# First FFN projection of two layers by Strassen's seven products for 18 of 22 chunks

## The chip, the cores and the metric

One core of a Trainium2 chip runs one program. TensorE (PE in the profile) multiplies matrices into PSUM; VectorE (DVE) and ScalarE (ACT) do elementwise work and can read PSUM; GpSimd (POOL) does elementwise work on SBUF; SyncE (SP) issues the DMAs. The metric is the device time of one execution in microseconds (us), as the median of several runs.

## The reference

A hybrid block of two layers is followed by a second block of two layers, all on 512 positions of width 1024. Each layer of the second block ends in the part that is changed, a feed-forward network (FFN) with a gated convolution:

```python
def conv_ffn(x, w_up, conv_w, conv_b, w_down):      # x 512x1024, w_up 1024x5632, w_down 2816x1024
    a, g = jnp.split(x @ w_up, 2, axis=-1)           # 2816 value columns, 2816 gate columns
    g = causal_depthwise_conv(g, conv_w) + conv_b    # 3 taps along the positions
    return (jax.nn.gelu(g) * a) @ w_down
```

## The kernel before

Every large product is made of three matmuls, since each operand is kept as a high and a low part: the high part is a copy in a rounded 32-bit format (`SC.copy`, ACT), the low part what is left over (`V.tensor_tensor` subtract, DVE). `split` does that for activations and `load_w` for weights: it loads a 128x512 tile `raw` by a DMA of SP's queue (4 buffers) and splits it into a slot `w`. There are 6 weight slots, and `more_w` adds 7 for the FFN, used in turn.

`ffn(l, ...)` is one layer's FFN. The activations stand transposed in `hT`: 8 tiles of 128 model columns by 512 positions, high and low. The 22 chunks of 128 gate columns and 128 value columns are worked in three parts of 8, 7 and 7 chunks, and inside a part in groups of up to four. For a group the gate's 8 weight tiles are loaded (`load_ws`, `K8`), and `fsteps` runs, for each chunk, 8 x 3 matmuls of 512 columns into one PSUM bank of `ps_mm` (4 buffers); then the same for the values. `ev_g` evacuates a gate chunk: ACT scales and adds the bias, DVE adds the two other taps of the convolution, ACT applies GELU. `ev_a` multiplies by the value chunk (DVE) and splits the result into `act` (ACT, DVE). The very first group of a layer runs its gate in two halves of 256 positions, so that it can begin while the last positions are still being normed; its three matmuls stand in lines 1517 to 1519, those of `fsteps` in lines 1060 to 1062.

After a part's groups comes its second projection: `down_part` multiplies `act` by the tiles of `w_down`, in `dsteps` (lines 231 to 233), for two column halves and four blocks of positions, and DVE adds the result to `z` (line 1532). The third part ends in the layer norm, whose rows `lng` and `lnb` are loaded by `rows`.

The instructions of each engine are put in order when the program is built, by a scheduler that follows the program's order where several could run; on the chip each engine then works through its list in that order. `tick`, `later` and `flush` place small pieces of other work between matmuls.

Of the kernel before, what the change touches and what calls it, by code (L numbers as in the profile page):

```python
# [20 lines left out]
S = 512  # L21
# [100 lines left out]
def _body(ctx, tc, nc, a, out, stop):  # L122
# [36 lines left out]
    def ps_t():  # L159
        return psum("t", [128, 4, 128], 2)  # L160
# [1291 lines left out]

    def open_z(l):
# [6 lines left out]
        def rows(i):  # L1460
            lg = [zp.tile([128, D], F32, name=n, bufs=1) for n in ("lng", "lnb")]
            bcast_row(lg[0], a["ln_g_2"][l, i])
            bcast_row(lg[1], a["ln_b_2"][l, i])
            return lg
        return st, z, rows

    def ffn(l, zst, z, rows, opf, est):
# [5 lines left out]
        more_w(f"wf{l}", 7, fst, "left")  # L1473
        cwr = fp.tile([88, 128], F32, name="cwr")
# [6 lines left out]
        for part, nch in enumerate((8, 7, 7)):  # L1481
            act = [fp.tile([128, 2, S], F32R, name="act", bufs=10) for _ in range(nch)]
            for q0 in range(0, nch, 4):
                nq = min(4, nch - q0)
                ge = {}

                def ev_g(j, ps):
                    c = c0 + q0 + j
                    g0 = fp.tile([128, S], F32, name="g0", bufs=2)
                    SC.activation(g0, ps, AF.Identity, scale=cw[:, 2, c:c + 1], bias=cw[:, 3, c:c + 1])  # L1490
                    V.scalar_tensor_tensor(g0[:, 1:], ps[:, :S - 1], cw[:, 1, c:c + 1], g0[:, 1:], op0=OP.mult, op1=OP.add)  # L1491
                    V.scalar_tensor_tensor(g0[:, 2:], ps[:, :S - 2], cw[:, 0, c:c + 1], g0[:, 2:], op0=OP.mult, op1=OP.add)
                    ge[j] = fp.tile([128, S], F32, name="ge", bufs=6)
                    SC.activation(ge[j], g0, AF.Gelu_apprx_tanh)
# [9 lines left out]
                if part == q0 == 0:  # L1504
                    pt = ps_t()
                    PE.transpose(pt[:, 0, :88], cwr, ident[:88, :88])
                    SC.copy(cw.rearrange("p a b -> p (a b)"), pt[:, 0, :88])
                    pss = [ps_mm() for _ in js]
                    for i, r in enumerate(halves):
                        for j, ps in enumerate(pss):  # L1510
                            for k in K8:
                                if i:
                                    flush()
                                else:
                                    tick()
# [560 lines left out]
```

## Time and profile before

| | |
|---|---|
| median of 3 runs | 1966.53 us (1961.64 to 1968.09) |
| profiled execution | 1962.12 us |
| its span, first to last instruction | 1960.3 us |
| mean granted clock of TensorE | 0.991 |
| matmuls | 10240 |
| busy: PE, DVE, ACT, POOL | 1899.6, 1167.4, 782.5, 203.2 us |
| DMA traffic | 206.18 MB, mean 105 GB/s |

The span is what the trace covers; 1.8 us of the execution's own time lie around it. The clock is a share of the full 2.4 GHz. Matmuls overlap, so the busy time of PE says that one was under way, not that PE ran at its peak.

### The profile page before, as it was taken

How to read it: one execution, taken by the hardware profiler on the slowest of the kernel's cores; microseconds unless marked ns; L12 is line 12 of the kernel's file. 1: busy time of each engine (PE TensorE's matmuls, PEld its weight loads, DVE VectorE, ACT ScalarE, POOL GpSimd, SP SyncE). 2: the span in 40 equal slices, each digit the busy share in tenths (PEclk: the TensorE clock that was granted, in tenths of full speed). 3: DMA queues.
4: the chain of work that ended last, by engine and by line, in shares of the span. 5: the costliest groups of instructions: out<-in, count | busy, mean ns of one | idle time of the engine just before them, and what ended most of it. 6: DMA issues, size and time to landing. Idle time of an engine off the chain costs nothing.

```text
span 1960.3 us, 29102 instructions
## 1 busy us (share of the span) xinstructions
PE 1899.6 (97%) x10240; PEld 1540.1 (79%) x10240; DVE 1167.4 (60%) x2892; ACT 782.5 (40%) x1760; POOL 203.2 (10%) x316
## 2 busy tenths in 40 slices
PE   7999899999999999999999999999999999999998
PEld 4777687877888888768888888888778788888886
DVE  5698887475774235687434444645776774344445
ACT  2432454432553345444323333234665543233330
POOL 3011102012101000110000000101441200000001
PEclk9999999989999999999999999999999999999999
DMA  8535425135234233404322332352113042223321
GB/s 275 170 91 179 130 86 160 58 109 155 65 103 143 65 94 118 162 1 128 94 86 86 108 98 85 112 168 86 42 41 130 24 129 92 86 87 107 99 86 69
DMA packets 132872, 206.18 MB, mean 105 GB/s; under 512 B 20866, under 2 KB 57076, under 8 KB 132725
## 3 DMA queue, kind: packets, MB, share of 16 engines
q1 hardware_dynamic: 132724, 204.31, 33.9%
q8 instruction: 81, 1.33, 0.3%
q14 instruction: 67, 0.54, 0.1%
HBM read 194.62 MB, written 14.09 MB: 106 GB/s over the span
## 4 chain that ended last, share of the span: by engine, by line
PE 72%; DVE 6%; POOL 2%; DMA 1%; issue 1%; ACT 1%; POOLq 0%; DVEq 0%; ACTq 0%
PE mm L1060 11%; PE mm L1062 11%; PE mm L1061 11%; PE mm L231 9%; PE mm L233 9%; PE mm L232 8%; PE t L1095 1%; PE t L274 1%; PE o L1854 1%; PE o L1662 1%; PE mm L1924 1%; DVE w L227 1%; DVE z L1152 1%; DMA raw<-in_ffn_w_up_dram 1%; PE o L939 1%
## 5 line engine op out<-in xcount | busy, mean ns | idle before, releaser
L226 ACT CAST w<-raw 128x512 fp32r<-128x512 f32 (+4 forms) x568 | 321.8, 581 | 401.2 <-PE mm L233 172.1
L227 DVE TENSOR_TENSOR w<-raw,w 128x512 fp32r<-128x512 f32 (+4 forms) x560 | 348.4, 643 | 174.4 <-ACT w L226 171.7
L1060 PE MATMUL mm<-hT,w 128*128 128x512 f32 x920 | 367.0, 399 | 0.0
L1062 PE MATMUL mm<-hT,w 128*128 128x512 f32 x920 | 362.4, 394 | 0.0
L1061 PE MATMUL mm<-hT,w 128*128 128x512 f32 x920 | 361.6, 393 | 0.0
L231 PE MATMUL mm<-w,hT 128*128 128x512 f32 (+3 forms) x704 | 278.2, 396 | 1.2 <-ACT hT L243 1.2
L233 PE MATMUL mm<-w,hT 128*128 128x512 f32 (+3 forms) x704 | 263.2, 374 | 0.0
L232 PE MATMUL mm<-w,hT 128*128 128x512 f32 (+3 forms) x704 | 261.5, 371 | 0.5 <-DVE w L227 0.5
L1062 PEld LDWEIGHTS mm<-hT,w 128*128 128x128 f32 x920 | 172.6, 188 | 40.0 <-DVE w L227 0.8
L1060 PEld LDWEIGHTS mm<-hT,w 128*128 128x128 f32 x920 | 172.9, 188 | 39.7 <-ACT w L226 1.1
L1061 PEld LDWEIGHTS mm<-hT,w 128*128 128x128 f32 x920 | 172.9, 188 | 36.1
L231 PEld LDWEIGHTS mm<-w,hT 128*128 128x128 f32 x704 | 139.8, 199 | 30.4 <-issue 6.9
L233 PEld LDWEIGHTS mm<-w,hT 128*128 128x128 f32 x704 | 139.8, 199 | 20.7 <-issue 1.1
L232 PEld LDWEIGHTS mm<-w,hT 128*128 128x128 f32 x704 | 140.1, 199 | 16.8 <-issue 1.8
L231 PE MATMUL mm<-w,act 128*128 128x512 f32 x352 | 139.0, 395 | 0.0
L232 PE MATMUL mm<-w,act 128*128 128x512 f32 x352 | 138.3, 393 | 0.0
L233 PE MATMUL mm<-w,act 128*128 128x512 f32 x352 | 138.2, 393 | 0.0
L1532 DVE SCALAR_TENSOR_TENSOR z<-z,mm 128x512 f32<-128x512 f32 x48 | 33.0, 687 | 109.8 <-PE mm L233 109.8
L1491 DVE SCALAR_TENSOR_TENSOR g<-mm,cw,g 128x511 f32<-128x511 f32 x44 | 33.0, 749 | 100.2 <-ACT g L1490 100.2
L281 POOL TENSOR_SCALAR rp<-mv 128x1 f32<-128x1 f32 x16 | 9.8, 614 | 775.9 <-DVE mv L1146 774.9
L1090 ACT ACTIVATE E<-E,nm 128x128 f32<-128x128 f32 (+3 forms) x128 | 71.6, 560 | 45.5 <-DVE nm L1089 42.8
L1497 DVE TENSOR_TENSOR ge<-ge,mm 128x512 f32<-128x512 f32 x44 | 30.2, 686 | 83.3 <-PE mm L1062 83.3
(433 smaller groups left out, 3060.0 us busy)
## 6 DMA issues: line engine op xcount, KB each, us to landing
raw<-in_ffn_w_up_dram SPq DMA_DIRECT2D x128, 256.0 KB, 2.9
rawm<-in_w_mod_dram SPq DMA_DIRECT2D x96, 256.0 KB, 3.1
raw<-in_ffn_w_down_dram SPq DMA_DIRECT2D x88, 256.0 KB, 3.0
raw<-in_w_in_dram SPq DMA_DIRECT2D x80, 256.0 KB, 2.8
raw<-in_ev_w_in_dram SPq DMA_DIRECT2D x48, 256.0 KB, 3.1
raw<-in_ffn_w_up_dram SPq DMA_DIRECT2D x64, 192.0 KB, 2.4
raw<-in_w_out_dram SPq DMA_DIRECT2D x32, 256.0 KB, 3.0
raw<-in_w_in_dram SPq DMA_DIRECT2D x32, 128.0 KB, 3.5
```

The costliest lines, as they stand in the source:

```text
L226: SC.copy(hi, r)
L227: (eng or V).tensor_tensor(lo, r, hi.bitcast(F32), op=OP.subtract)
L231: PE.matmul(ps, hi, w[:, 0, w0:w0 + n], start=first, stop=False)
L232: PE.matmul(ps, hi, w[:, 1, w0:w0 + n], start=False, stop=False)
L233: PE.matmul(ps, lo, w[:, 0, w0:w0 + n], start=False, stop=last)
L1060: PE.matmul(ps, wh, hi, start=k == ks[0], stop=False)
L1061: PE.matmul(ps, wh, lo, start=False, stop=False)
L1062: PE.matmul(ps, wl, hi, start=False, stop=k == ks[-1])
L1090: SC.activation(E, E, AF.Exp, scale=scale, bias=nm, accum_out=den)
L1491: V.scalar_tensor_tensor(g0[:, 1:], ps[:, :S - 1], cw[:, 1, c:c + 1], g0[:, 1:], op0=OP.mult, op1=OP.add)
L1497: V.tensor_tensor(ge[j], ge[j], ps, op=OP.mult)
L1532: V.scalar_tensor_tensor(hs, hs, R2 if part == 0 else 1.0, ps, op0=OP.mult, op1=OP.add)
```

## The change

The first projection of 18 of the 22 chunks of each layer is computed by quarters with Strassen's scheme. The model columns are halved (k tiles 0 to 3 and 4 to 7), the positions are halved (`LH`, `RH`), and the two column halves are a group's value columns and gate columns. Instead of eight products of quarters there are seven, each of four k tiles by 256 positions, so each product is 4 x 3 matmuls of 256 columns a chunk. They need sums of quarters on both sides.

On the activations' side `sums` builds three sums on DVE and splits them, once a layer, into the unused tile `yT` and a new tile `hx`; `scr` and `c1s` are views of the norm rows `lng` and `lnb` of the mixer before. On the weights' side, `up_quart` loads three of a group's four weight quarters as f32 (`s` and `x` in the four buffers `v0` to `v3`, `y` in four buffers `bq`), and makes the other operands in place: two sums by DMAs of POOL's queue that add while they write (`plus_dma`, and the one after `o3`), two by POOL (`y` plus `x`, and `plus_raw`, for which the fourth quarter is loaded into `raw`). Each of the seven operands is split into four weight slots.

The results are combined as the products end: the accumulator `X` (two banks of `ps_o`) takes products 0, 5, 6 and 3 in turn and is read in between, `W` and `Y` are two banks each of `ps_mm`. `e1` to `e7` are the evacuations; `e7` includes the gate's convolution and GELU (`gate`), `e4` the last product and the split into `act`. The order of products is 0, 1, 4, 5, 2, 6, 3; the last two run chunk by chunk (`byj`), the others k tile by k tile.

The first group of each layer stays as it was. The parts are 8, 8 and 6 chunks. To make room the FFN adds 3 weight slots for 7 and has 8 buffers of `act` for 10. The calls pass `lgs[0]`, the rows of the last norm.

```diff
-    def ffn(l, zst, z, rows, opf, est):
+    def ffn(l, zst, z, rows, lg0, opf, est):
         halves = (slice(0, 256), slice(256, 512))[::-1 if l else 1]
         fst = ExitStack()
         drain(opf)
         est.close()
         fp = pool(f"ff{l}", stack=fst, side="left")
-        more_w(f"wf{l}", 7, fst, "left")
-        cwr = fp.tile([88, 128], F32, name="cwr")
+        more_w(f"wf{l}", 3, fst, "left")
+        cwr = fp.tile([128, S], F32, name="g0", bufs=2)[:88, :128]
+        hx = fp.tile([128, 2, 4, S], F32R, name="hx")
+        scr = lg0[0].rearrange("p (k s) -> p k s", k=2)
+        c1s = [lg0[1][:, S * i:S * i + S].rearrange("p (j s) -> p j s", j=2) for i in range(2)]
         nc.sync.dma_start(cwr[0:66], a["ffn_conv_w_2"][l].rearrange("i (c p) -> (i c) p", p=128))
         nc.sync.dma_start(cwr[66:88], a["ffn_conv_b_2"][l].rearrange("(c p) -> c p", p=128))
         cw = fp.tile([128, 4, 22], F32, name="cw")
         up, down = a["ffn_w_up_2"][l], a["ffn_w_down_2"][l]
         c0 = 0
         st6 = {}
-        for part, nch in enumerate((8, 7, 7)):
-            act = [fp.tile([128, 2, S], F32R, name="act", bufs=10) for _ in range(nch)]
+        LH, RH = slice(0, 256), slice(256, 512)
+
+        def sums(k):
+            h0, l0, h1, l1 = (hT[:, q, kk:kk + 2] for kk in (k, 4 + k) for q in range(2))
+
+            def tt(o, x, y, op):
+                V.tensor_tensor(o, x, y, op=op)
+            t = scr
+            f = lambda v: v.bitcast(F32)
+            tt(t[:, :, LH], f(h1)[:, :, RH], f(h0)[:, :, RH], OP.subtract)
+            tt(t[:, :, RH], f(h0)[:, :, LH], f(h0)[:, :, RH], OP.subtract)
+            tt(t[:, :, LH], t[:, :, LH], f(l1)[:, :, RH], OP.add)
+            tt(t[:, :, RH], t[:, :, RH], f(l0)[:, :, LH], OP.add)
+            for c in (LH, RH):
+                tt(t[:, :, c], t[:, :, c], f(l0)[:, :, RH], OP.subtract)
+            split(yT[:, 0, k:k + 2], yT[:, 1, k:k + 2], t)
+            V.scalar_tensor_tensor(t[:, :, LH], t[:, :, LH], -1.0, f(h0)[:, :, LH], op0=OP.mult, op1=OP.subtract)
+            tt(t[:, :, LH], t[:, :, LH], f(l0)[:, :, LH], OP.subtract)
+            V.scalar_tensor_tensor(t[:, :, RH], t[:, :, LH], -1.0, f(h1)[:, :, LH], op0=OP.mult, op1=OP.subtract)
+            tt(t[:, :, RH], t[:, :, RH], f(l1)[:, :, LH], OP.subtract)
+            split(hx[:, 0, k:k + 2], hx[:, 1, k:k + 2], t)
+
+        SRC = ((hT, 0, LH), (hT, 4, LH), (hx, 0, RH), (hT, 4, RH), (yT, 0, LH), (hx, 0, LH), (yT, 0, RH))
...
+        def up_quart(q0, nq, act):
+            n, np2 = 128 * nq, nq // 2
+            cg = c0 + q0
+            col = (128 * cg, FF + 128 * cg)
+            src = {(i, m): (lambda k, i=i, m=m: up[128 * (4 * i + k):128 * (4 * i + k) + 128, col[m]:col[m] + n])
+                   for i in range(2) for m in range(2)}
+            buf = {}
+
+            def fresh(name, b):
+                for k in range(4):
+                    if name == "y":
+                        buf[name, k] = fp.tile([128, 512], F32, name="bq", bufs=4)[:, :n]
+                    else:
+                        buf[name, k] = vp.tile([128, 512], F32, name=f"v{k}", bufs=1)[:, :n]
+                    nc.sync.dma_start(buf[name, k], src[b](k))
+
+            def operand(name, then=None):
+                ws = []
+                for k in range(4):
+                    wturn[0] = (wturn[0] + 1) % len(wslots)
+                    px, nx = wslots[wturn[0]]
+                    w = px.tile([128, 2, 512], F32R, tag="w", name="w", bufs=nx)
+                    split(w[:, 0, :n], w[:, 1, :n], buf[name, k])
+                    ws.append(w)
+                    if then:
+                        then(k)
+                return ws
+
+            def plus_raw(k):
+                rw = wp.tile([128, 512], F32, tag="raw", name="raw", bufs=4)[:, :n]
+                nc.sync.dma_start(rw, src[1, 0](k))
+                GP.tensor_tensor(buf["y", k], buf["y", k], rw, op=OP.add)
+
+            X = [ps_o() for _ in range(np2)]
+            W, Y = [None] * np2, [None] * np2
+            g2 = [fp.tile([128, 2, S], F32, name="ge", bufs=3) for _ in range(np2)]
+            v3 = lambda ps: ps.rearrange("p (j s) -> p j s", j=2)
+
+            def product(i, ws, bank, start, byj, evac):
+                tile_, k0, cols = SRC[i]
+                order = [(k, j) for k in range(4) for j in range(nq)]
+                if byj:
+                    order = [(k, j) for jj in range(np2) for j in (2 * jj, 2 * jj + 1) for k in range(4)]
+                for k, j in order:
+                    jj = j // 2
+                    if start and k == 0 and j % 2 == 0 and bank[jj] is None:
+                        bank[jj] = ps_mm()
+                    tick()
+                    ps = bank[jj][:, 256 * (j % 2):256 * (j % 2) + 256]
+                    wh, wl = (ws[k][:, q, 128 * j:128 * j + 128] for q in range(2))
+                    hi, lo = (tile_[:, q, k0 + k, cols] for q in range(2))
+                    s0 = start and k == 0 and j % 2 == 0
+                    PE.matmul(ps, wh, hi, start=s0, stop=False, skip_group_check=True)
+                    PE.matmul(ps, wh, lo, start=False, stop=False, skip_group_check=True)
+                    PE.matmul(ps, wl, hi, start=False, stop=False, skip_group_check=True)
+                    if k == 3 and j % 2:
+                        evac(jj, v3(bank[jj]))
+
+            def e1(jj, ps):
+                SC.copy(c1s[jj], ps)
+
+            def e2(jj, ps):
+                V.tensor_tensor(c1s[jj], c1s[jj], ps, op=OP.add)
+
+            def e5(jj, ps):
+                SC.mul(g2[jj][:, :, RH], ps, -1.0)
+
+            def e6(jj, ps):
+                SC.mul(g2[jj][:, :, LH], ps, -1.0)
+
+            def e3(jj, ps):
+                V.tensor_tensor(g2[jj][:, :, LH], g2[jj][:, :, LH], ps, op=OP.subtract)
+
+            def e7(jj, ps):
+                V.tensor_tensor(g2[jj][:, :, RH], g2[jj][:, :, RH], ps, op=OP.subtract)
+                for j in range(2):
+                    gate(cg + 2 * jj + j, g2[jj][:, j], g2[jj][:, j])
+                V.tensor_tensor(g2[jj][:, :, LH], g2[jj][:, :, LH], c1s[jj], op=OP.mult)
+
+            def e4(jj, ps):
+                V.tensor_tensor(g2[jj][:, :, RH], g2[jj][:, :, RH], ps, op=OP.mult)
+                for j in range(2):
+                    d = act[q0 + 2 * jj + j]
+                    SC.copy(d[:, 0], g2[jj][:, j])
+                    V.tensor_tensor(d[:, 1], g2[jj][:, j], d[:, 0].bitcast(F32), op=OP.subtract)
+
+            fresh("s", (1, 0))
+            fresh("y", (0, 0))
+
+            def plus_dma(k):
+                GP.dma_start(buf["y", k], src[0, 1](k), accum_op=OP.add)
+            o1 = operand("y", plus_dma)
+            o2 = operand("s")
+            product(0, o1, X, True, False, e1)
+            fresh("x", (1, 1))
+            o5 = operand("y")
+            product(1, o2, W, True, False, e2)
+            for k in range(4):
+                GP.tensor_tensor(buf["y", k], buf["y", k], buf["x", k], op=OP.add)
+            o6 = operand("y", plus_raw)
+            product(4, o5, Y, True, False, e5)
+            o3 = operand("x", lambda k: GP.dma_start(buf["x", k], src[0, 1](k), accum_op=OP.add))
+            product(5, o6, X, False, False, e6)
+            o7 = operand("x")
+            product(2, o3, Y, False, False, e3)
+            o4 = operand("y")
+            product(6, o7, X, False, True, e7)
+            product(3, o4, X, False, True, e4)
+
+        def gate(c, ps, dst):
+            g0 = fp.tile([128, S], F32, name="g0", bufs=2)
+            SC.activation(g0, ps, AF.Identity, scale=cw[:, 2, c:c + 1], bias=cw[:, 3, c:c + 1])
+            V.scalar_tensor_tensor(g0[:, 1:], ps[:, :S - 1], cw[:, 1, c:c + 1], g0[:, 1:], op0=OP.mult, op1=OP.add)
+            V.scalar_tensor_tensor(g0[:, 2:], ps[:, :S - 2], cw[:, 0, c:c + 1], g0[:, 2:], op0=OP.mult, op1=OP.add)
+            SC.activation(dst, g0, AF.Gelu_apprx_tanh)
+
+        for part, nch in enumerate((8, 8, 6)):
+            act = [fp.tile([128, 2, S], F32R, name="act", bufs=8) for _ in range(nch)]
             for q0 in range(0, nch, 4):
                 nq = min(4, nch - q0)
-                ge = {}
+                if part or q0:
+                    up_quart(q0, nq, act)
+                    continue
+                g2 = [fp.tile([128, 2, S], F32, name="ge", bufs=3) for _ in range(2)]
+                ge = {j: g2[j // 2][:, j % 2] for j in range(4)}
 
...
                 drain(fsteps(load_ws(up, 128 * (c0 + q0), 128 * nq, K8), range(nq), h_rhs, ev_a))
+                for k in (0, 2):
+                    sums(k)
```

## Rows read from the trace of the kernel before

**Rows 1.** The page: span, and busy time of each engine

```profile
span 1960.3 us, 29102 instructions
...
PE 1899.6 (97%) x10240; PEld 1540.1 (79%) x10240; DVE 1167.4 (60%) x2892; ACT 782.5 (40%) x1760; POOL 203.2 (10%) x316
```

**Rows 2.** Windows: length, busy (count) of PE, PEld, DVE, ACT, POOL, clock, DMA share

```profile
889.00:923.00 34.00, 31.73 (x231) 30.09 (x230) 22.10 (x35) 15.89 (x28) 1.45 (x2) 0.95 0.45 132
...
1034.00:1111.00 77.00, 77.00 (x335) 62.61 (x334) 36.66 (x59) 29.83 (x52) 0.00 (x0) 1.00 0.31 93
1111.00:1150.00 39.00, 39.00 (x170) 31.67 (x169) 16.24 (x24) 9.51 (x16) 0.00 (x0) 1.00 0.32 99
```

**Rows 3.** Windows of TensorE alone, inside stages with one shape

```profile
912.00:920.00 8.00, 8.00 (x71) 1.00 0.41 129
...
946.00:982.00 36.00, 36.00 (x157) 1.00 0.32 95
```

**Rows 4.** TensorE groups by shape: xcount | busy us, mean ns | idle before

```profile
L1060 PE MATMUL mm<-hT,w 128*128 128x512 f32 x920 | 367.0, 399 | 0.0
...
L1517 PE MATMUL mm<-hT,w 128*128 128x256 f32 x128 | 36.5, 290 | 4.7 <-ACT w L226 4.6
```

**Rows 5.** Timeline (start us, duration, engine) at the end of a first projection

```profile
985.61 1.67 ACT L226 CAST w<-raw 128x512 fp32r<-128x512 f32 x3
...
986.43 1.89 DVE L227 TENSOR_TENSOR w<-raw,w 128x512 fp32r<-128x512 f32 x3
```

**Rows 6.** Groups of DVE instructions by shape, 922 to 1268

```profile
L227 DVE TENSOR_TENSOR w<-raw,w 128x512 fp32r<-128x512 f32 x95 | 63.7, 689 | 23.4 <-ACT w L226 22.9
...
L1500 DVE TENSOR_TENSOR act<-ge,act 128x512 fp32r<-128x512 f32 x22 | 15.2, 690 | 6.3 <-ACT act L1499 6.2
```

**Rows 7.** Timeline of one chunk's gate, ACT and DVE

```profile
950.60 0.78 ACT L1490 ACTIVATE g<-mm,cw 128x512 f32<-128x512 f32 x1 [1.25 <-PE mm L1062]
...
951.42 0.75 DVE L1491 SCALAR_TENSOR_TENSOR g<-mm,cw,g 128x511 f32<-128x511 f32 x1 [1.33 <-ACT g L1490]
...
952.20 0.75 DVE L1492 SCALAR_TENSOR_TENSOR g<-mm,cw,g 128x510 f32<-128x510 f32 x1
...
953.05 0.63 ACT L1494 ACTIVATE ge<-g 128x512 f32<-128x512 f32 x1 [1.66 <-DVE g L1492]
```

**Rows 8.** Groups of POOL instructions by shape, whole span

```profile
L704 POOL TENSOR_TENSOR d<-d,kF 128x256 f32<-128x256 f32 x14 | 10.9, 779 | 74.2 <-ACT d L702 60.9 <-DVE acc L390 6.3 <-DVE Sg L725 2.9
L1004 POOL TENSOR_TENSOR xo<-xo,sil_a 128x512 f32<-128x512 f32 x8 | 10.7, 1334 | 9.4 <-DVE sil_a L1003 9.4
L227 POOL TENSOR_TENSOR w<-raw,w 128x512 fp32r<-128x512 f32 x8 | 10.4, 1336 | 1.6 <-ACT w L226 1.6
```

**Rows 9.** Timeline around one POOL add beside DVE's work

```profile
601.65 1.63 POOL L1004 TENSOR_TENSOR xo<-xo,sil_a 128x512 f32<-128x512 f32 x1 [0.92 <-DVE sil_a L1003]
...
602.03 0.75 DVE L1005 SCALAR_TENSOR_TENSOR y<-mm,rstd,mod 128x512 f32<-128x512 f32 x1
...
602.69 1.13 DVE L227 TENSOR_TENSOR w<-raw,w 128x512 fp32r<-128x512 f32 x1
```

**Rows 10.** Groups of DVE instructions by shape, whole span: narrow splits

```profile
L227 DVE TENSOR_TENSOR w<-raw,w 128x256 fp32r<-128x256 f32 x48 | 19.8, 432 | 23.9 <-ACT w L226 23.5
```

**Rows 11.** DMA issues of the whole span, last column us to landing

```profile
raw<-in_ffn_w_up_dram SPq DMA_DIRECT2D x128, 256.0 KB, 2.9
...
skB<-rd SPq DMA_DIRECT2D x4, 192.0 KB, 6.5
```

**Rows 12.** Windows of TensorE around two waits for weights

```profile
1588.00:1596.00 8.00, 5.35 (x45) 1.00 0.65 221
...
908.20:911.70 3.50, 3.50 (x19) 0.51 0.51 133
```

**Rows 13.** Timeline of TensorE at those two waits

```profile
907.66 0.39 PE L1517 MATMUL mm<-hT,w 128*128 128x256 f32 x1 [1.98 <-ACT w L226]
...
1592.70 0.39 PE L1517 MATMUL mm<-hT,w 128*128 128x256 f32 x1 [2.65 <-ACT w L226]
```

More of the change, by code (lines that the diff above doesn't have):

```diff
@@ L1451, in out_evac @@
         return ev
+    lgs = [None]
     def open_z(l):
@@ L1460, in rows @@
         def rows(i):
-            lg = [zp.tile([128, D], F32, name=n, bufs=1) for n in ("lng", "lnb")]
+            lgs[0] = lg = [zp.tile([128, D], F32, name=n, bufs=1) for n in ("lng", "lnb")]
             bcast_row(lg[0], a["ln_g_2"][l, i])
@@ L1503, in ffn @@
                 js = range(nq)
[L1504 to L1515, printed above, removed]
-                                wh, wl = (ws[k][:, q, 128 * j:128 * j + 128] for q in range(2))
-                                PE.matmul(ps[:, r], wh, hT[:, 0, k, r], start=k == 0, stop=False)
-                                PE.matmul(ps[:, r], wh, hT[:, 1, k, r], start=False, stop=False)
-                                PE.matmul(ps[:, r], wl, hT[:, 0, k, r], start=False, stop=k == 7)
-                            if i:
-                                ev_g(j, ps)
-                    js = ()
-                drain(fsteps(ws, js, h_rhs, ev_g))
+                pt = ps_t()
+                PE.transpose(pt[:, 0, :88], cwr, ident[:88, :88])
+                SC.copy(cw.rearrange("p a b -> p (a b)"), pt[:, 0, :88])
+                pss = [ps_mm() for _ in js]
+                for i, r in enumerate(halves):
+                    for j, ps in enumerate(pss):
+                        for k in K8:
+                            if i:
+                                flush()
+                            else:
+                                tick()
+                            wh, wl = (ws[k][:, q, 128 * j:128 * j + 128] for q in range(2))
+                            PE.matmul(ps[:, r], wh, hT[:, 0, k, r], start=k == 0, stop=False)
+                            PE.matmul(ps[:, r], wh, hT[:, 1, k, r], start=False, stop=False)
+                            PE.matmul(ps[:, r], wl, hT[:, 0, k, r], start=False, stop=k == 7)
+                        if i:
+                            ev_g(j, ps)
                 drain(fsteps(load_ws(up, 128 * (c0 + q0), 128 * nq, K8), range(nq), h_rhs, ev_a))
+                for k in (0, 2):
+                    sums(k)
             def a_lhs(t, k):
@@ L2034, in _body @@
         return
-    ffn(0, zst, z, rows, opf, est)
+    ffn(0, zst, z, rows, lgs[0], opf, est)
     if stop == 4:
@@ L2044, in _body @@
         return
-    ffn(1, zst, z, rows, opf, mst)
+    ffn(1, zst, z, rows, lgs[0], opf, mst)
 _INS = ['x', 'c', 'positions', 'w_mod', 'b_mod', 'pre_norm_gain', 'post_norm_gain', 'w_in', 'attn_sinks', 'gla_gate_w',
```

8 lines of the change are left out of this document (1 added, 7 removed).

## Prediction, made before the changed kernel ran

> **What bounds the kernel now.** I read the page's head first: TensorE (PE) is busy 1899.6 of 1960.3 us [rows 1]. A busy PE can still be waiting between overlapping matmuls, so next come the windows of one FFN layer: in the first projection (1034 to 1111) and in the second (1111 to 1150) PE's busy time is the whole window, DVE is at 48% and 42%, ACT at 39% and 24%, POOL does nothing and the DMA engines are a third busy [rows 2]. So in these stages PE alone sets the pace and only fewer PE nanoseconds help, as long as nobody else becomes slower than PE. The reader is to see two paces there: in a stretch that holds only 512-column matmuls 157 of them touch 36.00 us, in one that holds only 256-column matmuls 71 touch 8.00 us [rows 3]. The windows count a matmul that only reaches in, so one duration is added (0.40 and 0.29 us [rows 4]): 36.40 / 157 = 0.232 and 8.29 / 71 = 0.117 us from start to start. The long stretch of rows 2 gives 77.40 / 335 = 0.231. A half-wide matmul costs half, its own weight load included. That matters, since the change makes all its matmuls half-wide.
>
> **PE: removed.** A chunk (128 gate and 128 value columns) is 48 matmuls of 512 columns before, 48 x 0.231 = 11.1 us. With seven products it is 7 x 4 x 3 = 84 of 256 columns, 84 x 0.117 = 9.8 us. A group of four falls from 44.4 to 39.2 us, one of two from 22.2 to 19.6. With 36 chunks in two layers PE's work falls by 36 x 1.28 = 46 us, 2.3%. The parts of 8, 8, 6 chunks for 8, 7, 7 leave the second projection's matmuls the same in number.
>
> **DVE: added.** From rows, back to back: three weight splits end after 1.89 us where one lasts 0.69, so 0.60 each [rows 5]; the other 512-wide tensor_tensor forms have the same mean [rows 6]; the two convolution steps of a chunk take 951.42 to 952.95, 1.53 us [rows 7]. A group of four had 16 splits, 4 products and 4 low parts: 24 x 0.60 + 4 x 1.53 = 20.5 us. Now it has 28 splits (seven operands of four tiles) and 14 others (e2 two, e3 two, e7 four, e4 six): 42 x 0.60 + 4 x 1.53 = 31.3 us, beside PE's 39.2. ACT goes to 28 x 0.53 for high parts [rows 5], 10 further copies or negations at about the same, and 4 x (0.78 + 0.63) for gate and GELU [rows 7]: 25.7 us, no bound.
>
> **POOL: added.** Eight adds of 128x512 a group. The nearest rows are such a two-input add at 1.33 us and POOL's own splits at 1.34 [rows 8], so 10.6 us, alone no bound. But an add and a DVE operation with two SBUF inputs don't run side by side: beside an add at 601.65 that ends at 603.28, the split started at 602.69 takes 1.13 for 0.69 us and ends 0.54 after it, while the DVE operation between them, which reads PSUM, keeps its 0.75 [rows 9]. The add itself takes 1.63 for its usual 1.3. Of DVE's 31.3 us the splits, the low parts, the c1 product and now the convolution too (its input is an SBUF tile where it was PSUM) have two SBUF inputs; only 8 x 0.60 = 4.8 us read PSUM. The split behaves as if it had begun when the add ended. So the price of the adds to DVE lies between 0 (all beside PSUM readers or an idle DVE) and 10.6 us (all in full); with the latter DVE and POOL need 31.3 + 10.6 = 41.9 us together, over PE's 39.2. I take that end less a little, since rows 9 show full exclusion and nothing milder.
>
> The Trainium skill, "SBUF — State Buffer", section "Who interferes with whom", states this as a rule: a Vector instruction with two SBUF inputs and a GpSimd one that reads SBUF exclude each other for a whole instruction. It speaks against giving the weight sums to POOL. By it the adds cost up to their whole 10.6 us; by the delay in rows 9 alone (1.13 for 0.69, 0.44 us a meeting) eight would cost 3.5 us and DVE, at 34.8, would stay under PE.
>
> So a group lasts those 41.9 us, less what overlaps, plus DVE's idle time that neither it nor POOL can use. Overlap I take as 1.9 us, since the adds lie in the middle products and e7 and e4, with half of the PSUM readers, at the end. Idle is sure to come. e7 of the first half can't start before half of product 6 (24 x 0.117 = 2.8 us), and one gate chain runs ACT, DVE, ACT from 950.60 to 953.68, 3.1 us [rows 7]. From mid product 6 to the group's end PE needs 8.4 us. DVE has e7 and e4 of both halves, 2 x (2 x 0.60 + 2 x 1.53) + 6 x 0.60 = 12.1 us, and the next operands: with 9 weight slots the three tiles after the first become free only as product 6 ends. Some 4 us of work are left then. A following group can't start its second bank (X is the accumulator to the last) and a following second projection waits for its last two act tiles. So I take 2.0 us of idle and 42.0 us a group: 2.4 saved of the 5.1. Bounds: 39.2 and 41.9 + 2.8 + 3.1 = 47.8.
>
> **The group of two** has 28 splits 256 wide, about 0.34 back to back (0.43 mean [rows 10] less the 0.09 by which two overlap in rows 5), 7 others at 0.60, two chains of 1.53: 16.8; eight 256-wide adds at 0.78 [rows 8] make 6.2. 23.0 us for 22.2 before: I take 1 us lost.
>
> **DMAs.** 24 transfers of 256 KB a group instead of 16; the engines were a third busy [rows 2]. SP's loads of y wait until the last operand has been split, two products (11 us) ahead, and land in 2.9 us [rows 11]; down loads queued behind them wait as long and have that cover too. The eight adding DMAs go through POOL's queue, each behind a split, with POOL's adds behind them. No such DMA is in the trace: a plain one of the size lands in 2.9, the slowest row in 6.5 us [rows 11]. From the first operand to the third there are two products, 11.2 us; four issues at an add's 1.3 us and 6.5 make 10.4. Nothing, at both ends; uncovered, each microsecond late costs one. The norm row that c1 occupies can be reloaded only after the last e7, in SP's queue ahead of down loads; it is used a whole second projection later, and the loads behind it wait less than the act tiles do: nothing.
>
> **The first group** stays plain, but has 9 slots for 13 and DVE's sums: 20 operations of 0.60 and four 1024-wide low parts of 1.2, 16.8 us a layer. Results are needed in the third product, and DVE is at 22.1 of 34 us in that window [rows 2], so they fit, narrowly: 2 us a layer, between 0 and 16.8.
>
> **The clock.** After an idle of 1.98 us at 905, PE waiting for a weight split, the granted clock was 0.51 from 908.2 to 911.7, that is the lower of its two levels (1.2 GHz), at a loss of 3.5 x 0.49 = 1.7 us; after 2.65 us at 1590 it stayed 1.00 [rows 12, 13]. Of ten ends of groups I let two fall: 3.4 us, between 0 and 17.
>
> **Sum.** 8 groups x -2.4 = -19.2, 2 x +1, 2 x +2, +3.4: -9.8 us. The profiled execution took 1962.1 us (1960.3 and 1.8 around it), so 1952.3; the median of the runs is 4.4 above that execution, so 1957.
>
> **Rivals.** *Cover is better*: adds fall into DVE's waits, groups are PE's 39.2 us and only 1 us is lost at each of ten ends: -46 + 10 + 4 = -32, 1935. For it: DVE's idle time of 8 us in such a group is nearly what the adds need.
> *The shared port decides, slower*: the adds exclude DVE in full and idle reaches 4.5 us, half-way to its bound: 46.4 us a group, 8 x 2.0 + 2 x 3 + 4 + 3.4 = +29, 1996. It turns at 44.4 - 41.9 = 2.5 us of idle without overlap: beyond that a group is slower than the plain one. For it: the end of a group is where DVE has 12 us of work in 8; against: POOL's adds are not due there, with a product or more of slack.
> *Adding DMAs land late*, at 13 us for four instead of 10.4, so each of ten groups waits some 2 us: -9.8 + 20 = +10, 1977. Against: both bounds stay under 11.2.
> *Clock falls at every end*: 17 for 3.4 us, -9.8 + 13.6 = +4, 1970: no change that can be told.
>
> **Chances.** Forecast (1948 to 1965) 0.42, cover better 0.17, port 0.22, late DMAs 0.10, clock 0.09. A measurement here can tell about 0.3%, 5.9 us. Faster: 0.30 of the forecast and the whole second case, 0.47. Same: 0.12 of the forecast, 0.04 of the port, 0.06 of the clock: 0.22. Slower: the rest, 0.31. Range 1932 to 1990: the better cover's centre and nearly the port's.
>
> **What would show it.** Right: 256-column matmuls at 0.117 us in groups; DVE over 75% busy there; splits at 1.1 us beside adds; PE idle at ends of groups, released by DVE's e4 products or by weight splits, some 3 us each, little inside. Wrong: PE waiting inside a group for splits that wait for adding DMAs or adds; sums holding up the first group; a half-clock stretch after each end; weight loads that no longer hide at half width.

## Result: slower by about 1.1%, where a gain of 0.5% was forecast

| | before | after |
|---|---|---|
| median of five runs each | 1965.0 us (1956.7 to 1968.1) | 1983.5 us (1980.1 to 1990.4) |
| ratio, 95% interval | | 1.0109 [1.0075, 1.0143] |
| profiled execution / its span | 1962.1 / 1960.3 us | 1983.5 / 1981.8 us |

The time lies inside the range (1932 to 1990) and on the other side of "before" from the forecast 1957.

**Where it went.** The head of the page after, to be set against [rows 1]:

```profile
span 1981.8 us, 32498 instructions
...
PE 1881.6 (95%) x11536; PEld 1584.9 (80%) x11536; DVE 1354.3 (68%) x3114; ACT 875.9 (44%) x1942; POOL 391.2 (20%) x476
```

PE is busy 18 us less and the span is 21.5 us longer: PE now waits. From the first gate matmul to the last matmul of the second projection the first layer takes 385.7 us (378.9 before) and the second 382.7 (372.7). That is 16.8 of the 21.5; 2.9 more lie after the last matmul (11.3 us, 8.4 before) and the rest ahead of and between the layers. The windows of the changed kernel's groups, columns as in [rows 2]: the lone group and the pair of the first layer, the pair of the second, and then four stretches inside that last pair's second group.

```profile
943.00:986.00 43.00, 40.62 (x337) 39.99 (x336) 32.09 (x40) 23.24 (x41) 16.34 (x12) 1.00 0.59 148
1031.00:1123.00 92.00, 83.78 (x674) 82.64 (x674) 69.54 (x90) 48.93 (x87) 36.63 (x28) 0.96 0.58 139
...
1727.00:1819.00 92.00, 82.91 (x668) 81.81 (x668) 68.89 (x89) 48.22 (x85) 36.62 (x28) 0.96 0.57 139
...
1795.00:1799.00 4.00, 4.00 (x36) 4.00 (x36) 0.00 (x1) 0.00 (x0) 2.37 (x3) 1.00 1.00 176
1799.00:1805.00 6.00, 0.47 (x5) 0.27 (x3) 2.13 (x4) 2.56 (x5) 0.00 (x0) 0.91 0.84 180
1805.00:1809.00 4.00, 3.54 (x16) 3.54 (x17) 3.20 (x6) 3.48 (x7) 0.00 (x0) 0.50 0.64 175
1809.00:1813.00 4.00, 4.00 (x29) 4.00 (x28) 2.87 (x5) 1.30 (x2) 0.00 (x0) 0.78 0.83 272
```

A pair takes 92 us where two plain groups took 88.8, and PE is busy in only 83 to 84 of them. The 36 matmuls in 4.00 us at 1795 are the pace when fed: 0.119 us a matmul with the one-duration correction of [rows 3, 4], 5.7 us a product, 40 us a group. Then PE stands still for 6 us, and for some 6 us more its clock is low: 0.50, the lower of its levels, then 0.78, which costs at most 4 x 0.50 + 4 x 0.22 = 2.9 us.

The waits of TensorE from 890 to 1975 (total us, times, longest) say on whom; L1562 is the first, L1564 the last of the three matmuls that a chunk makes with a weight tile:

```profile
PE o L1562 <- ACT ge L1578: 16.9, 8, 6.0
PE o L1562 <- DVE ge L1584: 7.9, 8, 1.1
PE o L1562 <- ACT w L243: 6.7, 2, 4.1
...
PE o L1564 <- DVE w L244: 2.4, 2, 1.6
PE mm L1562 <- ACT w L243: 2.2, 4, 0.9
PE mm L1564 <- DVE w L244: 1.5, 3, 0.6
```

37.6 us in all, of it 16.9 + 6.7 = 23.6 in front of product 6, which needs the seventh operand o7 and an accumulator that e6 (ACT, L1578) has read. The second group of the second layer's pair shows why it waits, from the timelines of POOL, ACT, DVE and PE:

```profile
1780.55 6.40 POOL L1608 TENSOR_TENSOR bq<-bq,v 128x512 f32<-128x512 f32 x4 [4.48 <-DMA v<-in_ffn_w_up_dram]
1786.91 6.93 POOL L1541 TENSOR_TENSOR bq<-bq,raw 128x512 f32<-128x512 f32 x4
1793.80 3.58 POOL L1611 DMA_DIRECT2D v<-in_ffn_w_up_dram  x4
...
1799.51 0.62 ACT L243 CAST w<-v 128x512 fp32r<-128x512 f32 x1 [8.84 <-DMA v<-in_ffn_w_up_dram]
...
1804.29 0.62 ACT L243 CAST w<-v 128x512 fp32r<-128x512 f32 x1 [0.62 <-DMA v<-in_ffn_w_up_dram]
1804.82 1.08 ACT L1578 ACTIVATE ge<-o 128x512 f32<-128x512 f32 x2
...
1789.22 5.78 DVE L244 TENSOR_TENSOR w<-v,w 128x512 fp32r<-128x512 f32 x4
...
1805.46 0.58 PE L1562 MATMUL o<-yT,w 128*128 128x256 f32 x1 [5.99 <-ACT ge L1578]
```

DVE splits o3 from 1789.22 to 1795.00; as each tile is split, its buffer may take its adding DMA. But POOL works its queue in order, and ahead of these DMAs stand the adds of `plus_raw`, until 1793.8. The four issues take 3.58 us, the landings come up to 1804.3, ACT splits o7 as they land, and e6 waits in ACT's queue behind those splits although its product had ended at 1793.8. The names "ACT" and "e6" in the wait are thus the last link of a chain that runs back to POOL.

Two views of this group alone, of o3's splits (shortest, median and longest in ns) and of x's four adding DMAs, say what the raw adds do to these DMAs:

```profile
L244 DVE TENSOR_TENSOR w<-v,w x4: 680/1776/1780, 1789.2 to 1794.3; 128x512 fp32r<-128x512 f32 x4
...
DMA to landing us min/median/max: 5.6/7.6/8.7
```

The raw adds hold the first DMA in POOL's queue for 2.8 us after its tile has been split, but the last for only 0.5, since o3's last tile is not split before 1795.0. That is late because three of the four splits, beside the raw adds, take 1.78 us and not 0.68. So the raw adds delay the DMAs in two ways, ahead of them in the queue and beside the splits. From the first issue to the last landing the four then take 10.4 us, and product 2 ends 5.7 us after the first issue. The chain does not begin with the raw adds either: POOL stood idle for 4.48 us before its first add, until x's plain load had landed, and SP could issue that only as the second operand, in the same buffers, was split.

The sizes, from the groups by shape (xcount | busy us, mean ns of one) and the DMA issues (xcount, KB, median us to landing) of the whole span:

```profile
L244 DVE TENSOR_TENSOR w<-bq,w 128x512 fp32r<-128x512 f32 x128 | 123.1, 993 | 36.7 <-ACT w L243 35.4 <-PE mm L1564 0.3
L244 DVE TENSOR_TENSOR w<-v,w 128x512 fp32r<-128x512 f32 x96 | 76.7, 824 | 51.1 <-ACT w L243 51.0
L1541 POOL TENSOR_TENSOR bq<-bq,raw 128x512 f32<-128x512 f32 x32 | 55.0, 1750 | 0.0
L1608 POOL TENSOR_TENSOR bq<-bq,v 128x512 f32<-128x512 f32 x32 | 49.2, 1562 | 45.8 <-DMA v<-in_ffn_w_up_dram 40.2 <-DVE w L244 5.6
L1611 POOL DMA_DIRECT2D v<-in_ffn_w_up_dram x40 | 36.0, 1188 | 1.0 <-DVE w L244 0.9
```

```profile
bq<-in_ffn_w_up_dram POOLq DMA_DIRECT2D x32, 256.0 KB, 4.7
v<-in_ffn_w_up_dram POOLq DMA_DIRECT2D x32, 256.0 KB, 6.0
```

Adds take 1.56 and 1.75 us (1.33 in [rows 8]) and splits 0.82 to 0.99 (0.69 in [rows 6]). An adding DMA lands in a median of 4.7 to 6.0 us (2.9 for a plain one in [rows 11]) and costs POOL 36.0 / 40 = 0.90 us to issue.

### The profile page after: what moved, and what is told of

Read it like the earlier page. It is cut to its first block, busy times and chain, and to the rows that moved or that the text cites. A ratio compares the mean times of both kernels' runs of the same rounds, so it can differ in the third digit from the quotient of the medians.

```text
span 1981.8 us, 32498 instructions
## 1 busy us (share of the span) xinstructions
PE 1881.6 (95%) x11536; PEld 1584.9 (80%) x11536; DVE 1354.3 (68%) x3114; ACT 875.9 (44%) x1942; POOL 391.2 (20%) x476
## 4 chain that ended last, share of the span: by engine, by line
PE 51%; DVE 14%; DMA 7%; POOL 5%; issue 4%; ACT 3%; SPq 0%; ACTq 0%; POOLq 0%; DVEq 0%
PE mm L231 7%; PE mm L233 7%; PE mm L232 7%; DMA v<-in_ffn_w_up_dram 5%; PE mm L1060 4%; PE mm L1062 4%; PE mm L1061 4%; DVE w L244 2%; PE t L1095 1%; DVE w L227 1%; POOL bq L1541 1%; DVE g L1622 1%; DMA raw<-in_ffn_w_down_dram 1%; DVE g L1623 1%; PE t L274 1%
## 5 line engine op out<-in xcount | busy, mean ns | idle before, releaser
L227 DVE TENSOR_TENSOR w<-raw,w 128x512 fp32r<-128x512 f32 (+4 forms) x400 | 252.2, 649 | 121.0 <-ACT w L226 119.6
L226 ACT CAST w<-raw 128x512 fp32r<-128x512 f32 (+4 forms) x408 | 231.7, 581 | 214.4 <-PE mm L233 80.4
L244 DVE TENSOR_TENSOR w<-bq,w 128x512 fp32r<-128x512 f32 (+1 forms) x160 | 138.4, 895 | 40.0 <-ACT w L243 38.4
L232 PEld LDWEIGHTS mm<-w,hT 128*128 128x128 f32 x704 | 140.3, 199 | 16.8 <-issue 2.1
L243 ACT CAST w<-bq 128x512 fp32r<-128x512 f32 (+1 forms) x160 | 87.7, 578 | 130.6 <-PE mm L233 57.4
L1060 PE MATMUL mm<-hT,w 128*128 128x512 f32 x344 | 141.1, 411 | 0.0
L1062 PE MATMUL mm<-hT,w 128*128 128x512 f32 x344 | 135.5, 396 | 0.1
L1061 PE MATMUL mm<-hT,w 128*128 128x512 f32 x344 | 135.0, 394 | 0.0
L244 DVE TENSOR_TENSOR w<-v,w 128x512 fp32r<-128x512 f32 (+1 forms) x120 | 89.8, 775 | 61.0 <-ACT w L243 60.7
L1600 POOL DMA_DIRECT2D bq<-in_ffn_w_up_dram x40 | 35.1, 972 | 420.3 <-DVE w L244 324.7
L243 ACT CAST w<-v 128x512 fp32r<-128x512 f32 (+1 forms) x120 | 66.6, 575 | 94.8 <-DMA v<-in_ffn_w_up_dram 79.6
L1562 PE MATMUL o<-hT,w 128*128 128x256 f32 x288 | 82.2, 285 | 8.0 <-DVE ge L1584 7.9
```

Of the source, the lines that this page charges most:

```text
L226: SC.copy(hi, r)
L227: (eng or V).tensor_tensor(lo, r, hi.bitcast(F32), op=OP.subtract)
L232: PE.matmul(ps, hi, w[:, 1, w0:w0 + n], start=False, stop=False)
L243: SC.copy(hi, ps)
L244: V.tensor_tensor(lo, ps, hi.bitcast(F32), op=OP.subtract)
L1060: PE.matmul(ps, wh, hi, start=k == ks[0], stop=False)
```

## Experiments

Twelve kernels. The ratio is that of the runs to the kernel before on the same chip. "Stages" is the sum of both layers' stretches, measured in each trace as above, less the 751.6 us of before: it leaves out what varies elsewhere. It is one execution each; e5's profiled one was 7.4 us under the median of its runs and e1's 2.7 over.

```
kernel                                      median us   ratio [95%]               stages, us
after                                       1983.5      1.0109 [1.0075, 1.0143]    +16.8
e1  x's DMAs ahead of the raw adds          1962.4      1.0002 [0.9981, 1.0023]     -1.8
e2  all sums by adding DMAs                 1972.5      1.0048 [1.0025, 1.0072]     +3.7
e3  POOL's eight adds left out              1941.1      0.9879 [0.9855, 0.9903]    -25.3
e5  e6 ahead of o7's splits                 1974.2      1.0039 [1.0014, 1.0065]     +5.3
f2  e1 and e5                               1958.5      0.9975 [0.9952, 0.9997]     -7.5
f1  e1, e2 and e5                           1982.2      1.0093 [1.0069, 1.0117]    +17.0
f4  f2, groups of two plain                 1946.8      0.9918 [0.9893, 0.9944]    -18.3
e4  x's adding DMAs left out                1938.1      0.9878 [0.9849, 0.9908]    -32.1
g1  x's DMAs plain, same queue              1950.7      0.9951 [0.9932, 0.9970]     -9.5
g2  x's DMAs plain, SP's queue              1955.2      0.9960 [0.9930, 0.9991]    -12.8
g3  the last two sums change places         1944.0      0.9913 [0.9887, 0.9939]    -23.6
g5  g3, e5, plain two, order of 6 and 3     1933.4      0.9866 [0.9842, 0.9891]    -32.8
```

The **queue theory**: x's DMAs are late because of what stands ahead of them in POOL's queue, and everything behind o7 waits. Its rivals as a cause of the loss: the ends of groups, as the forecast had it; the exclusion between POOL's adds and DVE's splits; the landing time of an adding DMA.

### e1, e2, e3, e5: one suspect each

e1 puts the four raw adds behind x's DMAs in POOL's queue:

```diff
-            o6 = operand("y", plus_raw)
+            o6 = operand("y")
             product(4, o5, Y, True, False, e5)
             o3 = operand("x", lambda k: GP.dma_start(buf["x", k], src[0, 1](k), accum_op=OP.add))
+            last = nc.cur_bb.bb.instructions[-1]
+            with tc.issue_after(last):
+                for k in range(4):
+                    plus_raw(k)
```

> Only the order in POOL's queue changes: a group's four adding DMAs into x stand ahead of its four adds of the fourth quarter (plus_raw) instead of behind them. Queue theory (POOL works in order; the DMAs wait there behind adds that DVE's splits stretch to 1.77 us, so o7 is late and product 6 waits): the waits before and inside product 6, some 38 us over the ten groups, mostly go; 1945 to 1960 us. Landing theory (the adding DMA itself, 5.6 us, is too slow wherever it is issued): part of the wait stays, 1965 to 1975. End-of-group theory (DVE's gate and last product set the loss): 1975 to 1985.

e2 makes the other sums by adding DMAs too:

```diff
-                rw = wp.tile([128, 512], F32, tag="raw", name="raw", bufs=4)[:, :n]
-                nc.sync.dma_start(rw, src[1, 0](k))
-                GP.tensor_tensor(buf["y", k], buf["y", k], rw, op=OP.add)
+                GP.dma_start(buf["y", k], src[1, 0](k), accum_op=OP.add)
...
-                GP.tensor_tensor(buf["y", k], buf["y", k], buf["x", k], op=OP.add)
+                GP.dma_start(buf["y", k], src[1, 1](k), accum_op=OP.add)
```

> All four weight sums of a group are made by adding DMAs; POOL adds nothing, so no add shares DVE's SBUF port and nothing but DMA issues stands in POOL's queue. Queue theory: 1940 to 1955 us, splits of DVE back at 0.60 us. Landing theory: y now passes three adding DMAs in series and x one, so it gets worse, 1985 to 2000. End-of-group theory: 1972 to 1983.

e3 leaves out those eight adds and the loads that feed `plus_raw`:

```diff
-                rw = wp.tile([128, 512], F32, tag="raw", name="raw", bufs=4)[:, :n]
-                nc.sync.dma_start(rw, src[1, 0](k))
-                GP.tensor_tensor(buf["y", k], buf["y", k], rw, op=OP.add)
+                pass
...
-            for k in range(4):
-                GP.tensor_tensor(buf["y", k], buf["y", k], buf["x", k], op=OP.add)
```

> POOL's eight adds a group and the load for four of them are left out, so two operands are not the sums that they should be; the adding DMAs stay. Queue theory: the x DMAs go out right behind their splits, 1935 to 1950 us, about as with every sum by DMA. Landing theory: as before, 1975 to 1985. End-of-group theory: 1975 to 1983.

e5 moves e6 ahead of o7's splits in ACT's queue:

```diff
-            o7 = operand("x")
+            neg = [i for i in nc.cur_bb.bb.instructions if i.engine == mybir.EngineType.Activation][-1]
+            with tc.issue_after(neg):
+                o7 = operand("x")
```

> Only ACT's order changes: e6, which product 6 waits for since both use the accumulator X, is put ahead of the splits of o7. Theory of ACT's order (e6 is held up behind splits that wait for DMAs, and that alone makes product 6 late, as the releaser named in the waits says): 1955 to 1965 us. Queue theory: product 6 needs all four tiles of o7 for its first chunk anyway, so no change, 1979 to 1985.

e1 takes back 19 us of stages and e3 42. Only e3's time is inside the queue theory's range. e1 and e5 came out between their cases, and e2 inside the case of the ends of groups, which e3 rules out. In e3 the pair runs at PE's pace, 81 us, with DVE at 69%:

```profile
1618.00:1658.00 40.00, 38.94 (x328) 38.74 (x327) 24.77 (x41) 21.89 (x40) 4.17 (x5) 1.00 0.57 138
1704.00:1785.00 81.00, 80.46 (x674) 79.94 (x673) 56.20 (x89) 48.60 (x86) 10.46 (x12) 1.00 0.56 131
```

The end of a group then costs next to nothing, which takes the forecast's idle off the list. e2 shows that the adds alone are not it: it has none, its splits are back at 0.69 us, and 29 us of e3's gain are missing. Its splits over the whole span, then o3's splits, x's DMAs and their landing in the second group of the second layer's pair:

```profile
L244 DVE TENSOR_TENSOR w<-bq,w 128x512 fp32r<-128x512 f32 x128 | 85.7, 690 | 68.4 <-ACT w L243 68.2
...
1781.50 2.49 DVE L244 TENSOR_TENSOR w<-v,w 128x512 fp32r<-128x512 f32 x4
...
1782.48 3.83 POOL L1609 DMA_DIRECT2D v<-in_ffn_w_up_dram  x4
...
DMA to landing us min/median/max: 5.9/6.9/9.0
```

There o3's splits take 2.49 us, each of x's DMAs goes out 0.3 us behind its split, and PE still waits 3.2 us in front of product 6. What differs from e3 is the landing, 9.0 us for the last (6.9 in e3), and that o3's splits start 1.7 us into product 5 (1.5 us ahead of it in e3). The same views of e1:

```profile
1780.97 2.48 DVE L244 TENSOR_TENSOR w<-v,w 128x512 fp32r<-128x512 f32 x4
...
1782.86 3.58 POOL L1611 DMA_DIRECT2D v<-in_ffn_w_up_dram  x4 [4.17 <-DVE w L244]
...
DMA to landing us min/median/max: 3.9/5.8/8.2
```

With the raw adds behind, o3's splits are back at 2.48 us for four, and POOL stands idle for them. So e1 takes away both ways in which the raw adds delay x's DMAs, as e3 does, and no run here separates the two: that the place in the queue alone was the loss is not shown.

e5 gained 11.5 us of stages (9.3 by the medians), where the queue theory, as first put, had expected nothing. A wait at ACT's splits is then met inside product 6, tile by tile (10.5 us and more for that product in second groups of pairs), and no longer in front of it with e6 behind. The order of ACT's queue was a loss of its own.

### f2, f1, f4: the orders together

f2 is e1 and e5 in one kernel, f1 adds e2's edit. f4 is f2 with the groups of two computed by the plain path:

```diff
-                if part or q0:
+                if (part or q0) and nq == 4:
                     up_quart(q0, nq, act)
                     continue
...
                 js = range(nq)
+                if q0:
+                    drain(fsteps(ws, js, h_rhs, ev_g))
+                    drain(fsteps(load_ws(up, 128 * (c0 + q0), 128 * nq, K8), js, h_rhs, ev_a))
+                    continue
```

> e1 and e5 together: the adding DMAs of x are issued ahead of the raw adds in POOL's queue, and ACT takes e6 ahead of the splits of the seventh operand. POOL's eight adds stay. If the two orders are separate losses (e1 gave 21 us, e5 9 us against the changed kernel), 1983 - 21 - 9 = 1953 us. If ACT's order costs only because the seventh operand is late (queue theory), e1 has taken that already and this stays at e1's 1962. If POOL's adds themselves, stretched by DVE's splits, set the pace (sums of y late, the fourth operand behind them), also 1960 to 1965, with the wait in front of the last product.

> All twelve more sums of a group by adding DMAs, x's ahead of y's last four, and e6 ahead of the seventh operand's splits: no POOL add is left. Queue theory: with the right order nothing is late, groups of four near 40 us as without the adds (e3, 1941), so 1942 to 1950. Landing theory (an adding DMA needs 5.5 us and some 1 us of issue on POOL each, and y's three sums are a chain): the fifth operand of the chain stays late, waits of 2 to 3 us a group remain, 1960 or more.

> f2 with the groups of two (one in each layer) computed plainly, with 512-column matmuls, as in the kernel before. In the changed kernel such a group takes 29 to 30 us against 22.2 plain, so if that loss does not depend on the orders this is 14 us under f2; if the orders have already cured it, up to 5 us over or under f2 (a plain group of two has 2.6 us more of TensorE work).

f2 fell between its two cases: e5's 11.5 us are worth 5.7 on top of e1. f4's plain groups of two are worth 10.8 us of stages, 5.4 each. f1 came out in the range of its second case, slow landing (1960 or more), and undid every gain. Its waits of TensorE (1635 to 1990), and DVE's and PE's timeline at one of them:

```profile
PE o L1560 <- DVE ge L1582: 14.1, 6, 4.5
```

```profile
1807.40 0.69 DVE L244 TENSOR_TENSOR w<-bq,w 128x512 fp32r<-128x512 f32 x1 [0.15 <-ACT w L243]
...
1808.61 0.68 DVE L1582 TENSOR_TENSOR ge<-ge,o 128x512 f32<-128x512 f32 x1
...
1809.43 0.55 PE L1560 MATMUL o<-hT,w 128*128 128x256 f32 x1 [4.46 <-DVE ge L1582]
```

The four DMAs for o4 now go out last and land in 7.0 us (median of all 96 on y), o4's splits wait for them, and e7 (L1582), which product 3 needs, stands behind those splits in DVE's queue. The lateness was handed from one in-order queue to the next.

### e4, g1, g2: x's four transfers

e4 leaves x's adding DMAs out, g1 makes them plain loads at the same place in POOL's queue, g2 plain loads by SP.

```diff
 e4  o3 = operand("x")
 g1  o3 = operand("x", lambda k: GP.dma_start(buf["x", k], src[0, 1](k)))
 g2  o3 = operand("x", lambda k: nc.sync.dma_start(buf["x", k], src[0, 1](k)))
```

> The four adding DMAs on x are left out (the seventh operand is then the third over again, so the output lacks that sum); POOL's adds stay as they are. If the late landing of these DMAs is the loss, all waits in front of product 6 go: 1955 to 1963, as e1 or a little better. If the adds stretch DVE's splits so far that DVE sets the pace, groups stay at 43 us or more: 1973 or more.

> The four adding DMAs on x become plain loads of the same block, at the same place in POOL's queue (the seventh operand lacks the sum). Nothing but the landing changes. If the place in the queue, behind the raw adds, is the loss, some 10 us of the waits in front of product 6 stay when landing is 2.9 us shorter: 1960 to 1970. If the adding itself is slow and the place does not matter: 1938 to 1945, as with these DMAs left out (e4).

> The same four plain loads through SP's queue, not POOL's (the seventh operand lacks the sum). Queue theory: nothing stands ahead of them but the third operand's splits, 1938 to 1945 as e4. If their bytes on the DMA engines, or a wait that holds SP's later loads, were the loss: 1955 or more.

e4, at 1938 us below both of its cases, settles whether the exclusion sets the pace of a group. Its eight adds take 1.55 and 1.77 us, its splits 0.82 and 1.00, as in the changed kernel, DVE is at 86% of a pair, and yet the pair takes 81 us:

```profile
1702.00:1783.00 81.00, 80.49 (x674) 80.09 (x674) 69.41 (x90) 49.50 (x87) 29.78 (x21) 1.00 0.49 133
```

Against e3 the adds cost DVE 69.41 - 56.20 = 13.2 us in a pair, 6.6 a group, and the pair no time. The 48.9 us of stages between e4 and the changed kernel are for the most part found in the latter's 37.6 us of waits (4.5 in the same lines of e4) and at most some 12 us of low clock (1.00 less the granted clock, over the two pairs at 0.96 and the two last parts at 0.98 and 0.95: 3.7 + 3.7 + 1.4 + 3.5; some of it fell while PE stood still and is in the waits already). So x's four adding DMAs, as they are placed, are the loss, and not the adds and the exclusion by themselves, which e4 keeps.

g1 prices the adding: issue falls to 22.2 / 40 = 0.56 us and landing to 4.1.

```profile
L1611 POOL DMA_DIRECT2D v<-in_ffn_w_up_dram x40 | 22.2, 560 | 2.6 <-DVE w L244 1.9
```

```profile
v<-in_ffn_w_up_dram POOLq DMA_DIRECT2D x32, 256.0 KB, 4.1
```

That is 26 us of stages, and 22.6 are left against e4. The time lies between the two cases: neither the late issue nor the adding is the whole; both eat the same slack. The Trainium skill, "DMA: Bandwidth & Descriptors", section "SWDGE vs HWDGE vs iDMA", says that a transfer which accumulates can only be issued from GpSimd; in this kernel all of them are, and no run shows another way.

g2 came out at its upper case. SP's queue is in order too: x's loads stand behind loads of the second projection's weights, and those wait for buffers that the raw adds hold; o3's splits, beside the raw adds, are as late as before. SP's waits from 1755 to 1792:

```profile
SPq L213 <- POOL bq L1541: 14.2, 4, 10.3
```

### g3, g5: the same work, the sums changed about

If slack is the matter, the sum with the tightest due time should have the shortest way. In g3 o4's sum, wanted last, is made by adding DMAs and o7's by POOL adds of a block that SP loads early: the same eight adds, eight adding DMAs and bytes.

```diff
 def plus_raw(k):
-    rw = wp.tile([128, 512], F32, tag="raw", name="raw", bufs=4)[:, :n]
-    nc.sync.dma_start(rw, src[1, 0](k))
-    GP.tensor_tensor(buf["y", k], buf["y", k], rw, op=OP.add)
+    GP.dma_start(buf["y", k], src[1, 0](k), accum_op=OP.add)
+def x_raw(k):
+    rw = wp.tile([128, 512], F32, tag="raw", name="raw", bufs=4)[:, :n]
+    nc.sync.dma_start(rw, src[0, 1](k))
+    GP.tensor_tensor(buf["x", k], buf["x", k], rw, op=OP.add)
...
-o3 = operand("x", lambda k: GP.dma_start(buf["x", k], src[0, 1](k), accum_op=OP.add))
+o3 = operand("x", x_raw)
```

g5 adds e5's order and the plain group of two, and products 6 and 3 take each weight tile for both chunks of a pair before the next:

```diff
-order = [(k, j) for jj in range(np2) for j in (2 * jj, 2 * jj + 1) for k in range(4)]
+order = [(k, j) for jj in range(np2) for k in range(4) for j in (2 * jj, 2 * jj + 1)]
```

> The two sums change places: y's last sum (for the fourth operand, wanted last) is made by adding DMAs, issued as the sixth operand is split, and x's sum (for the seventh operand, wanted two products after the third) by POOL adds of a block loaded early. The same number of adds, adding DMAs and bytes. Queue theory: the tight sum has the short way and the long way has two products of slack, so groups of four near 40 us, the group of two still late: 1945 to 1955. If the amount of POOL work, or the exclusion between its adds and DVE's splits, is the loss: 1975 or more, as nothing of that changes.

> The swap, e6 ahead of the seventh operand's splits in ACT, the two group of two plain, and products 6 and 3 that take the four weight tiles in turn for a pair of chunks. If each of these is a separate loss: groups of four at 40 us or a little under, 8 x 40 + 2 x 22.4 against 2 x 222 before, 1930 to 1940. If the swap has taken all: within 4 us of the swap less the group of two's 7 us a layer.

g3 is 40 us of stages faster than the changed kernel with nothing removed. POOL's timeline in the same group (its adding DMAs are now L1544, its adds for o7 L1541), and the pair's window:

```profile
1754.89 6.39 POOL L1611 TENSOR_TENSOR bq<-bq,v 128x512 f32<-128x512 f32 x4 [5.49 <-DMA v<-in_ffn_w_up_dram]
1761.22 3.58 POOL L1544 DMA_DIRECT2D bq<-in_ffn_w_up_dram  x4
1764.48 2.88 POOL L1541 TENSOR_TENSOR v<-v,raw 128x512 f32<-128x512 f32 x2
1768.00 3.37 POOL L1541 TENSOR_TENSOR v<-v,raw 128x512 f32<-128x512 f32 x2 [0.64 <-DVE w L244]
```

```profile
1703.00:1785.00 82.00, 80.37 (x670) 79.69 (x669) 70.47 (x88) 48.87 (x85) 35.52 (x28) 1.00 0.62 156
```

x's sums are done at 1771.4, ahead of product 6 at 1772.8; the DMAs for o4 have until 1778.6. At 1944.0 us g3 is just under the queue theory's range and far from the 1975 of its rival; it shows that the amount of adds and their exclusion are not the loss by themselves. What stays are the groups of two (5.6 us of waits for e6). g5, inside the ranges of both its cases, is faster than both kernels, 0.9866 of before; which of its three additions beside the plain groups of two gave what was not separated. In g5 e7 still holds product 3 for 2.7 us in three waits.

## Why the prediction was wrong

**The step that failed** is the DMA paragraph: "Nothing, at both ends", with 10.4 us for four issues and a landing against 11.2 of slack. The price held: from the first issue to the last landing x's four took 8.8 to 10.4 us in the eight groups of four. (Four issues of 1.3 us and 6.5 are 11.7, over the slack; 10.4 is right for three issues ahead of the last DMA, whose landing counts from its own start.) The slack was not there: from the first issue to the end of product 2 it was 5.7 and 5.8 us in the two groups with the long waits and 7.9 to 10.6 in the other six, where 11.2 was forecast. What the working left out is when the first DMA can go: it wrote that each adding DMA goes "behind a split, with POOL's adds behind them". That holds for y's four. Ahead of x's four stand the four raw adds, 6.93 us of POOL in the group shown, and beside o3's splits, which must come first, the same adds make three of four 1.78 us long. Two further queues passed the lateness on, ACT's (e6 behind o7's splits) and, in f1, DVE's. The rival "adding DMAs land late" had the place right and, at 2 us a group for ten groups, nearly the waits in front of product 6, 23.6 us; its reason, a dearer landing, was not the one. e4 measures the price of x's four, clock included, at 48.9 us. That the time lies inside the range is luck: the upper end came from the port's case, and the term that decided stood at nothing.

**DVE and POOL as the floor of a group: wrong.** 41.9 us a group was the sum of DVE's and POOL's work under full exclusion. The exclusion itself is real: splits 0.99 for 0.69 us beside adds, 0.69 in e2 without them. The Trainium skill, "SBUF — State Buffer", section "Who interferes with whom", has it as an exclusive lock, and these durations agree. But its price is 6.6 us a group on DVE, of 10.6, and e4 runs groups in 40 us with it. The rival "shared port decides" falls as a floor of the group; what the exclusion did do was to make o3's splits, and with them x's DMAs, late.

**PE's share: right.** A fed matmul takes 0.119 us (forecast 0.117), a fed group of four 40 us (39.2), and weight loads hide at half width. Of 5.1 us a group 4.4 can be had: 8 x 4.4 = 35, and g5 gets 32.8 over both layers. The rival "cover better", 1935, is close to what the kernel does when its sums come in time and its groups of two are plain (g5, 1933).

**Ends of groups: mis-placed.** Forecast 2.0 us of idle at each, released by e4 or weight splits. Measured: up to 1.1 us at eight places, and in front of product 3, released by e7; the large waits are inside, in front of product 6, which is what the forecast had named as its own refutation.

**Group of two: mis-sized.** 1 us lost was forecast. f4 puts it at 5.4 us each against f2. With half the matmuls a product lasts 24 x 0.119 = 2.9 us, so the same chain of issue, landing and split has half the cover (the waits of 6.7 us for ACT's splits, shown above, are those of the two groups of two); the cost was taken from DVE's and POOL's work and not from that chain.

**First group: cheaper than forecast.** 2 us lost a layer were forecast. The first two groups together take 90.0 and 93.4 us (94.9 and 95.7 before), and the second has only 1.4 and 0.2 of that (43.0 and 44.2 for 44.4): the sums hold nothing up. The first group itself is 3.5 and 2.1 us shorter because the waits of [rows 13], 1.98 and 2.65 us, and the low clock behind the first of them, 1.7 us [rows 12], are gone: its gate's matmuls (now L1659 to L1661) wait 1.2 us in both layers together, and the granted clock there is 1.00. Why the splits come earlier there is not shown.

```profile
PE mm L1661 <- DVE w L227: 1.2, 3, 0.8
```

**Clock: mis-sized, and elsewhere.** 3.4 us at ends of groups was forecast; at most some 12 us follow the waits inside groups, and none remain in the pairs where the waits are gone (granted clock 1.00 in e3, e4, g3).

## What to carry to other kernels

Before costing a transfer or a sum at nothing, write out the in-order queue it is issued from, with what stands ahead of it at that moment, and when the buffer that it writes comes free; count the slack from there. A resource that is half idle can still be late. When an operand has two ways of being made, give the one with the least slack the short way and the one wanted last the long one: this alone was worth 40 us here, with the same number of adds, adding DMAs and bytes. A wait's named releaser (here e6) may only be what was queued last: follow it back through every engine that was itself waiting.

## Not expected of the hardware

- An adding DMA of 256 KB costs POOL 0.90 us to issue and lands in a median of 6.0 us; a plain one at the same place 0.56 and 4.1 (g1); 2.9 from SP's queue [rows 11]. With 96 such DMAs on y and 32 on x the medians were 7.0 on y and 6.0 on x (f1), or 5.4 and 7.0 (e2). Of four issued 0.6 us apart the last took 8.7 us to land.
- POOL adds beside splits take 1.56 to 1.75 us for 1.33, and splits 0.82 to 0.99 for 0.69: both sides pay, where [rows 9] had suggested one split a meeting. Where adds follow each other, each split beside them lasts as long as an add (1.78 us beside 1.75).
- A wait of 6.0 us was followed by 4 us at a granted clock of 0.50 and 4 us at 0.78, at most 2.9 us lost, which is half as much again as the wait itself.
